# Sums over chunks in the FFN's down product, seeded in PSUM, in a two-layer diffusion backbone

## Chip, cores and metric

One Trainium2 chip, one core of it. The metric is device time in microseconds, the median of three runs; lower is better.

## What is computed

The input is a latent sequence of 512 tokens and a context of 256, both 1024 wide. Two layers run over them: an FFN half-step, a mixing of tokens (two kinds of attention and a Fourier mixing between an input and an output projection), and another FFN half-step. The same weights act on context and latent tokens; only the latent tokens are the output, so the last FFN leaves the context out. The FFN, to which the change belongs:

```python
def swiglu(h, w1, w2):
    gate, up = jnp.split(h @ w1, 2, axis=-1)
    return (jax.nn.silu(gate) * up) @ w2

def ffn_sublayer(h, m, sub, g_pre, g_post, w1, w2):
    shift, scale, gate = mods_of(m, sub)
    y = swiglu(modulate(rms_norm(h, g_pre[sub]), shift, scale), w1, w2)
    return h + MACARON_WEIGHT * gate * rms_norm(y, g_post[sub])
```

The inner width is 2816. `shift`, `scale` and `gate` come from a product of a conditioning vector with `w_mod` (1024 x 9216 in each layer).

## The kernel before

All matrix products run in three parts: both operands are split into a rounded high part and the rest, and high x high, high x rest and rest x high are added in PSUM (`mm`, L690 to L699). So each weight tile costs a copy on ScalarE (ACT; `wh`, L324) and a subtraction on VectorE (DVE; `wl`, L328) after its load.

The FFN takes its 22 pairs of 128 inner columns in seven chunks (`CHUNKS`: six of 3 pairs and one of 4). For each pair it computes gate and up. Two or three pairs of an FFN run plainly (`pair`); the others (`pair7`) form a two-by-two block product from seven products instead of eight, in three banks A, B and E. Between those products ACT copies a bank to SBUF (`copy`, L935) before the next product may go on in it, and DVE adds the pieces up (L941, L948, L968). After the pairs of a chunk and one more pair come the chunk's down products (`down`): for each tile of 128 tokens and each half of the output (12 tiles, or 8 without the context) 3 x 3 matmuls of 512 columns into one bank. Then `yacc` adds the bank to the tile y in SBUF: for the first chunk a copy on ACT (L1021), for the others an add on DVE (L1023). In the last chunk the tiles go on to the norm and the next stage (`chain`).

The modulation vectors are made beside all this: `mods` loads `w_mod` in 128 pieces (raw<-wmodT, L427) and multiplies them on DVE (L433), one or two products for each piece. When the eight pieces of a gate are done, `make_post` writes it as a row to DRAM (gsd<-gs, L533), element by element; from there it is read back as a broadcast. Loads of weights (raw<-w) and of w_mod (raw<-wmodT) and these rows are all issued by SyncE and share its DMA queue. The three `raw` buffers hold the loads until they are split or multiplied.

The order of all instructions is made ahead, when the kernel is built. `Sched` plays generators against a small model of the engines: an `op` occupies an engine for a given time, a `wait` waits for an event, an `acq` takes a slot of a counted resource (banks are `pb`, 8 of them; weight slots `w`), lower `prio` goes first where two could start together. `S.busy[engine]` is the time up to which an engine is occupied in that account. The order that it finds is what each engine's queue holds; on the chip an engine works it off in that order, and waits where something is not ready yet. A bank is a new tile of an eight-buffer pool each time (`bank`, L262).

Of the kernel before, what the change touches and what calls it, by code (L numbers as in the profile page):

```python
# [10 lines left out]
F32 = mybir.dt.float32  # L11
# [29 lines left out]
SCALE_ACT = 0.2  # L41
HALVES = ((1, 1),)
# [140 lines left out]
class Prog:  # L183
# [5 lines left out]
    def setup(self, es):  # L189
# [10 lines left out]
        self.pb = pool("pb", 8, space=PSUM)  # L200
# [3 lines left out]
        cp = self.cp  # L204

# [56 lines left out]
    def bank(self):  # L262
        p = self.pb.tile([128, 512], F32, name="b")
        return p
# [177 lines left out]
    def first_mods(self):  # L442
# [28 lines left out]
        def finish(j, ps):  # L471
            row = self.qp.tile([128, 512], F32, name="q")
            yield op("act", t_act(512), lambda: nc.scalar.activation(row[:4, :], ps[:4, :], AF.Copy))
            S.rel("pb")
# [11 lines left out]
            if j == 3:  # L486
                S.rel("pb")
# [77 lines left out]
    def chain(self, gi, src, post, pre, out=False):  # L565
# [86 lines left out]
        def split(j, bank):  # L652
# [10 lines left out]
            S.rel("pb")  # L663
# [48 lines left out]
    def ffn(self, l, f, streams, nxt):  # L712
# [19 lines left out]
        def evac(i, parts):  # L732
# [8 lines left out]
            def part(gate, up, banks, lo, n, ready, e):  # L741
# [4 lines left out]
                S.rel("pb", banks)  # L746
# [20 lines left out]
        def parts2(ps, ready):  # L767
            out = [(*ps["l"], 2, NC, NL, ready["l"], Event())]
            if has_c:
                out.append((*ps["c"], 1, 0, NC, ready["c"], Event()))  # L770
            return out
# [145 lines left out]
        def pair7(i):  # L917
# [6 lines left out]
            def out():  # L924
# [13 lines left out]
                def silu(h, src, p):  # L938
# [3 lines left out]
                    S.rel("pb")  # L942
# [3 lines left out]
                def store(h, up):  # L946
                    yield wait(gate[h])
                    yield op("dve", t_dve(N), lambda: nc.vector.tensor_tensor(ts[h], ts[h], up, ALU.mult))  # L948
                    S.rel("q" if h else "pb")
# [61 lines left out]

        ydone = {}

        def yacc(t, h, p, c, e, prio=None):
# [9 lines left out]
            S.rel("pb")  # L1024
            S.set(e)

        def down(c):
# [4 lines left out]
            def part(bank, t, h, ks, rel):  # L1032
                for k in ks:
                    w = yield wait(self.W["w2", l, f, c0 + (n * h + k) // 2][(n * h + k) % 2])
                    gt = [x[:, t * 128 : t * 128 + 128] for x in g[c0 + k]]
                    yield op("pe", 3 * t_mm(512), lambda: self.mm([bank], gt, [w], k == 0, k == n - 1))
                    if rel:
                        S.rel("w")

            for i in range(c0, min(c0 + n, NPAIR - 1)):  # L1040
                yield wait(gdone[i])
            if not last:
                for h in range(2):
                    for t in tiles:
                        yield acq("pb")
                        bank = self.bank()
                        yield from part(bank, t, h, range(n), t == tiles[-1])
                        S.spawn(yacc(t, h, bank, c, Event()), 2)
            else:
# [5 lines left out]
                first = [(t, h) for t in tiles[:2] for h in range(2)]  # L1055
                banks = {}
                for th in first:
                    yield acq("pb")
                    banks[th] = self.bank()
                    yield from part(banks[th], *th, range(n - 1), False)  # L1060
                for t in tiles:
                    yield wait(last_half[t % 2])
                    for h in range(2):
                        if (t, h) in banks:
                            yield from part(banks[t, h], t, h, [n - 1], False)
                        else:
                            yield acq("pb")
                            banks[t, h] = self.bank()
                            yield from part(banks[t, h], t, h, range(n), t == tiles[-1])
                        S.spawn(yacc(t, h, banks[t, h], c, evs[t, h]), 1 + 0.01 * t)  # L1070
# [3 lines left out]
        for c in range(len(CHUNKS)):  # L1074
            need = sum(CHUNKS[: c + 1])
            while made < min(need + 1, NPAIR):
                if made == NSTD[2 * l + f]:
# [3 lines left out]
            yield from down(c)  # L1081


    def mix(self, l, ctx_out, nxt):
# [27 lines left out]
        def evac(name, pl, pc, rels):  # L1112
# [10 lines left out]
            for r in rels:  # L1123
                S.rel(r)
            T[name] = t
            if n2 in ("av", "bv"):
                offs = [0, 128] + [NC + o for o in ((0, 128, 256, 384, 64, 192, 320) if n2 == "av" else (0, 128, 256, 384))]
                dst = self.va[:, :, int(name[2]) * 128 : int(name[2]) * 128 + 128] if n2 == "av" else self.vb
                for i in range(0, len(offs), 3):
# [7 lines left out]
                    S.rel("pb")  # L1137
# [21 lines left out]
        def u_split(c, outs):  # L1159

            for src, lo, hi in reversed(list(zip(outs, (NC, 0), (NT, NC)))):
# [4 lines left out]
                S.rel("pb")  # L1166
# [23 lines left out]
        def fnet():  # L1190
# [19 lines left out]
            def ab_split(tt, pb, e):  # L1210
# [3 lines left out]
                S.rel("pb")  # L1214
# [37 lines left out]
            S.rel("pb")  # L1252
            freed(0, 1)

            def unfold(s, c, h, a0, P, Q, banks):
# [7 lines left out]
                S.rel("pb", banks)  # L1263
                yield from out_split(s, 6 + c, f, ["q"])

            for s, i, h, tts, n in streams:
# [6 lines left out]
                for c in range(2):  # L1273
                    banks = 1 if s == "c" else 2
                    yield acq("pb", banks)
                    p = self.bank()
# [578 lines left out]
```

## Time and profile before

| | us |
|---|---|
| median of three runs | 2559.97 |
| lowest, highest | 2559.94, 2564.85 |
| the profiled execution | 2558.9 |
| its span (first to last instruction) | 2557.1 |

| engine | busy, us | share of the span |
|---|---|---|
| PE (TensorE, matmuls) | 2497.7 | 98% |
| DVE (VectorE) | 1956.6 | 77% |
| ACT (ScalarE) | 1265.7 | 49% |

Two matmuls overlap at their ends, so a busy PE is not a PE at its peak; what it lost shows as idle time, as a wait or as a lower granted clock. "b" is a bank, "g" the inner activations, "hh" and "hl" the two parts of the normed input, "x" tiles hold block sums. A line such as `ACT q L935 <- ...` names the engine, the tile that is written and the line of the kernel.

### The profile page before, as it was taken

Reading aid. Unit: us, or ns where it says so; the run is one execution under the profiler, and the core shown is the slowest. Engines: PE = TensorE matmul, PEld = TensorE weight load, DVE = VectorE, ACT = ScalarE, POOL = GpSimd, SP = SyncE. Lnnn points to the kernel's source line nnn. Section 1 sums busy time; section 2 is a strip of 40 time slices with the busy share of each in tenths; the row PEclk is TensorE's granted clock in tenths of the full one; section 3 lists DMA queues with packets and bytes.
Section 4 is the critical chain, followed back from the end, with each engine's and each line's share of the span. In section 5 each row is a group of like instructions: output and inputs, shape, how many; then the busy total and the mean of one; then the engine's idle time right before and its main releaser. Section 6 shows DMA issues by size and latency. Waiting matters only on the chain.

```text
span 2557.1 us, 40296 instructions
## 1 busy us (share of the span) xinstructions
PE 2497.7 (98%) x15304; PEld 2282.2 (89%) x15304; DVE 1956.6 (77%) x3906; ACT 1265.7 (49%) x2529; POOL 68.4 (3%) x136
## 2 busy tenths in 40 slices
PE   7999999999998999998999999999999999999998
PEld 5989998998887999998999999999999888899998
DVE  7878888876888397887887978666667686777887
ACT  8443333356657474333334643333347666654544
POOL 0000000010000000000000100000001000000000
PEclk9999999999999999999999999999999999999999
DMA  7344434353321334344447354222243222333333
GB/s 257 95 121 124 125 122 102 123 194 106 124 63 35 124 100 131 114 126 107 125 125 203 118 156 154 77 75 66 75 140 127 68 70 75 115 108 91 102 105 132
DMA packets 100931, 294.17 MB, mean 115 GB/s; under 512 B 20608, under 2 KB 27136, under 8 KB 100608
## 3 DMA queue, kind: packets, MB, share of 16 engines
q1 hardware_dynamic: 100736, 291.59, 37.1%
q8 instruction: 120, 1.97, 0.3%
q14 instruction: 75, 0.61, 0.1%
HBM read 274.73 MB, written 16.82 MB: 114 GB/s over the span
## 4 chain that ended last, share of the span: by engine, by line
PE 90%; DVE 4%; DMA 3%; ACT 2%; issue 1%; POOL 0%; SPq 0%; DVEq 0%; POOLq 0%; ACTq 0%
PE b L693 83%; PE b L1348 2%; PE b L1391 2%; PE b L1324 2%; DMA raw<-wmodT 1%; PE b L675 1%; DMA raw<-w 1%; DVE wl L328 1%; ACT wh L324 1%; DMA raw<-win 1%; DVE q L433 0%; DVE wl L460 0%; DVE g L1299 0%; ACT y L661 0%; PE b L499 0%
## 5 line engine op out<-in xcount | busy, mean ns | idle before, releaser
L693 PE MATMUL b<-hh,wh 128*128 128x256 f32 (+2 forms) x2184 | 702.6, 322 | 18.2 <-ACT q L935 12.6
L693 PE MATMUL b<-hl,wh 128*128 128x256 f32 (+2 forms) x2184 | 686.0, 317 | 1.9 <-DVE hl L668 1.6
L693 PE MATMUL b<-hh,wl 128*128 128x256 f32 (+2 forms) x2184 | 666.7, 318 | 0.0
L693 PE MATMUL b<-wh,g 128*128 128x512 f32 x1936 | 606.7, 390 | 0.0
L328 DVE TENSOR_TENSOR wl<-raw,wh 128x512 fp32r<-128x512 f32 x553 | 366.7, 688 | 128.8 <-ACT wh L324 126.5
L324 ACT ACTIVATE wh<-raw 128x512 fp32r<-128x512 f32 x553 | 336.3, 627 | 231.7 <-PE b L693 178.5
L693 PEld LDWEIGHTS b<-hh,wh 128*128 128x128 f32 x2184 | 413.8, 189 | 40.1 <-ACT q L935 13.5
L693 PEld LDWEIGHTS b<-wh,g 128*128 128x128 f32 x1936 | 363.5, 188 | 73.9
L693 PEld LDWEIGHTS b<-hl,wh 128*128 128x128 f32 x2184 | 413.7, 189 | 14.6 <-DVE hl L668 2.8
L693 PEld LDWEIGHTS b<-hh,wl 128*128 128x128 f32 x2184 | 401.6, 189 | 3.0
L324 ACT ACTIVATE wh<-q 128x512 fp32r<-128x512 f32 x308 | 190.6, 629 | 417.7 <-DVE y L1023 248.9
L693 PE MATMUL b<-wl,g 128*128 128x512 f32 x968 | 377.1, 390 | 0.0
L433 DVE CUSTOM_DVE_ANT_0 q<-raw,cb 128x1024 bf16<-128x1024 f32 x224 | 273.3, 1220 | 56.4 <-DMA raw<-wmodT 55.9
L693 PE MATMUL b<-x,wh 128*128 128x384 f32 (+1 forms) x1232 | 292.3, 323 | 0.0
L328 DVE TENSOR_TENSOR wl<-q,wh 128x512 fp32r<-128x512 f32 x308 | 206.2, 687 | 73.2 <-ACT wh L324 72.0
L1023 DVE TENSOR_TENSOR y<-y,b 128x512 f32<-128x512 f32 x264 | 179.4, 684 | 100.9 <-PE b L693 99.3
L693 PEld LDWEIGHTS b<-x,wh 128*128 128x128 f32 x1232 | 215.1, 189 | 0.0
L693 PEld LDWEIGHTS b<-wl,g 128*128 128x128 f32 x968 | 181.7, 188 | 36.0
L693 PE MATMUL b<-x,wl 128*128 128x384 f32 (+1 forms) x616 | 198.5, 322 | 0.0
L693 PE MATMUL b<-g,wh 128*128 128x384 f32 (+1 forms) x616 | 147.8, 325 | 3.5 <-ACT s L935 3.5
L961 ACT ACTIVATE g<-s 128x384 fp32r<-128x384 f32 (+1 forms) x154 | 75.5, 494 | 95.2 <-DVE s L948 94.0
L693 PEld LDWEIGHTS b<-x,wl 128*128 128x128 f32 x616 | 116.1, 189 | 0.0
(258 smaller groups left out, 3186.5 us busy)
## 6 DMA issues: line engine op xcount, KB each, us to landing
raw<-w SPq DMA_DIRECT2D x264, 512.0 KB, 3.7
raw<-wmodT SPq DMA_DIRECT2D x128, 512.0 KB, 3.6
raw<-win SPq DMA_DIRECT2D x32, 512.0 KB, 3.6
spill<-x SPq DMA_DIRECT2D x28, 512.0 KB, 2.9
x<-spill SPq DMA_DIRECT2D x26, 512.0 KB, 7.0
g<-wmod SPq DMA_DIRECT2D x32, 256.0 KB, 5.4
raw<-wout SPq DMA_DIRECT2D x16, 512.0 KB, 3.6
y<-bias SPq DMA_DIRECT2D x24, 256.0 KB, 3.2
```

The lines of the kernel that those rows point to most:

```text
L324: yield op("act", t_act(512), lambda: nc.scalar.activation(w[0], src, AF.Copy))
L328: yield op("dve", t_dve(512), lambda: nc.vector.tensor_tensor(w[1], src, w[0].bitcast(F32), ALU.subtract))
L433: yield op("dve", t_dve(1024, True), lambda: nc.vector.tensor_tensor_reduce(junk, raw, self.cb[:, i, :], 1.0, 0.0, ALU.mult, ALU.add, self ...
L675: r = nc.tensor.transpose(bank[:, c : c + 128], yb[:, t, 2 * j + i, :], self.ident)
L693: mm = lambda *a, **k: self.nc.tensor.matmul(*a, skip_group_check=onto, **k)
L961: yield op("act", t_act(N), lambda: nc.scalar.activation(gh, ts[h], AF.Copy))
L1023: yield op("dve", t_dve(512), lambda: nc.vector.tensor_tensor(dst, dst, p, ALU.add))
L1324: r = nc.tensor.transpose(pb[:, j * 128 : j * 128 + 128], P[:, b * 128 : b * 128 + 128], self.ident)
L1348: r = nc.tensor.matmul(ps[b][:, c : c + w], lhsT=q[x], rhs=k[x], start=first, stop=final, skip_group_check=True)
L1391: r = nc.tensor.matmul(po["t"][64 * h : 64 * h + 64, cols], lhsT=vs[h][j], rhs=Ps[h][:, j * 128 : j * 128 + 128], start=(j == 0), stop=(j ...
```

## The change

The sum over chunks goes through the bank. A generator `begin` runs ahead of the down products, at most two tiles (four in the last chunk): it takes a bank and, from the second chunk on, lets ACT copy y's part into it. The first matmul then adds to the bank's content, without its start flag. Afterwards the bank holds the sum and is copied to y, by ACT or by DVE. A tile is seeded only where ACT's account is at most 1.5 us (`ACT_MORE`) ahead of DVE's, and only in a bank that the down products have written in full before (`full`); otherwise the add on DVE stays. `plan` starts `begin` ahead of the last pair that precedes a chunk's down products.

The eight banks are made once and given out from a list of free ones: the down products prefer banks that are full, all others those that are not, in order of the time at which they came free. All places that gave back a count now give back the bank itself (`drop`); these lines are left out of the diff below.

```diff
+ACT_MORE = 1.5
-        self.pb = pool("pb", 8, space=PSUM)
+        self.pb = pool("pb", 1, space=PSUM)
...
+        self.banks = [self.pb.tile([128, 512], F32, name=f"b{i}") for i in range(8)]
+        self.bank_of = {b.tensor.name: i for i, b in enumerate(self.banks)}
+        self.free = [(0.0, i) for i in range(8)]
+        self.full = [False] * 8
...
-    def bank(self):
-        p = self.pb.tile([128, 512], F32, name="b")
-        return p
+    def bank(self, full=False):
+        self.free.sort(key=lambda e: (self.full[e[1]] != full, e))
+        i = self.free.pop(0)[1]
+        if not full:
+            self.full[i] = False
+        return self.banks[i]
+
+    def drop(self, *aps):
+        t = self.S.cur.t
+        for a in aps:
+            self.free.append((t, self.bank_of[a.tensor.name]))
+        self.S.rel("pb", len(aps))
...
+        def begin(c, order, look, evs):
+            for t, h in order:
+                yield acq(look)
+                yield acq("pb")
+                bank = self.bank(True)
+                i = self.bank_of[bank.tensor.name]
+                seeded = c > 0 and self.full[i] and S.busy["act"] <= S.busy["dve"] + ACT_MORE
+                if seeded:
+                    yield wait(ydone[t, h])
+                    yield op("act", t_act(512), lambda: nc.scalar.activation(bank, self.y[t][:, h * 512 : h * 512 + 512], AF.Copy))
+                self.full[i] = True
+                S.set(evs[t, h], (bank, seeded))
...
             if c == 0:
                 yield wait(y_free)
+            if c > 0 and not seeded:
+                yield op("dve", t_dve(512), lambda: nc.vector.tensor_tensor(dst, dst, p, ALU.add))
+            elif S.busy["act"] <= S.busy["dve"] + ACT_MORE:
                 yield op("act", t_act(512), lambda: nc.scalar.activation(dst, p, AF.Copy))
             else:
-                yield op("dve", t_dve(512), lambda: nc.vector.tensor_tensor(dst, dst, p, ALU.add))
-            S.rel("pb")
+                yield op("dve", t_dve(512), lambda: nc.vector.tensor_copy(dst, p))
+            self.drop(p)
...
+        def plan(c):
+            if c < len(CHUNKS) - 1:
+                order = [(t, h) for h in range(2) for t in tiles]
+            else:
+                order = [(t, h) for t in tiles for h in range(2)]
+            look = ("look", l, f, c)
+            S.res[look] = Res(2)
+            evs = {th: Event() for th in order}
+            S.spawn(begin(c, order, look, evs), 2)
+            return order, look, evs
...
-                    yield op("pe", 3 * t_mm(512), lambda: self.mm([bank], gt, [w], k == 0, k == n - 1))
+                    yield op("pe", 3 * t_mm(512), lambda: self.mm([bank], gt, [w], k == 0 and not seeded, k == n - 1, seeded))
                     if rel:
                         S.rel("w")
+                if ks[-1] == n - 1:
+                    S.rel(look)
...
+                S.rel(look, 2)
...
             while made < min(need + 1, NPAIR):
+                if made == min(need, NPAIR - 1):
+                    planned = plan(c)
```

## Rows read from the trace of the kernel before

**Rows 1.** The page: the span and the engines' busy time.

```profile
span 2557.1 us, 40296 instructions
...
PE 2497.7 (98%) x15304; PEld 2282.2 (89%) x15304; DVE 1956.6 (77%) x3906; ACT 1265.7 (49%) x2529; POOL 68.4 (3%) x136
```

**Rows 2.** Busy time by stretch: PE, PEld, DVE, ACT, POOL, then clock, DMA, GB/s.

```profile
250.40:318.80 68.40, 68.40 (x363) 64.14 (x362) 58.06 (x101) 25.57 (x48) 0.00 (x0) 1.00 0.41 123
250.40:276.80 26.40, 26.40 (x121) 22.22 (x120) 22.38 (x38) 5.02 (x9) 0.00 (x0) 1.00 0.32 100
276.80:318.80 42.00, 42.00 (x243) 41.92 (x242) 35.69 (x64) 20.56 (x40) 0.00 (x0) 1.00 0.47 138
...
2341.00:2387.30 46.30, 46.30 (x326) 43.43 (x325) 37.40 (x69) 22.90 (x48) 0.00 (x0) 1.00 0.34 102
```

**Rows 3.** The adds of L1023: ns min/median/max, first start; busy in one stretch.

```profile
L1023 DVE TENSOR_TENSOR y<-y,b x264: 677/684/690, 184.4 to 2549.8; 128x512 f32<-128x512 f32 x132
...
250.40:276.80 26.40, 7.53 (x11) 1.00 0.32 100
```

**Rows 4.** PE's waits, whole span: us in total, times, longest.

```profile
PE b L693 <- ACT q L935: 12.6, 3, 6.6
```

**Rows 5.** Busy time by stretch, as in rows 2, around three waits.

```profile
165.00:185.00 20.00, 15.62 (x77) 14.79 (x76) 11.21 (x21) 6.68 (x15) 0.00 (x0) 0.91 0.56 164
420.00:440.00 20.00, 16.48 (x86) 16.16 (x86) 17.26 (x30) 7.63 (x15) 0.00 (x0) 0.91 0.42 129
1200.00:1220.00 20.00, 13.38 (x68) 13.06 (x67) 16.64 (x28) 6.57 (x13) 0.00 (x0) 0.83 0.40 110
```

**Rows 6.** The chain of waits before each of the four: start, duration, what.

```profile
164.38 9.88 DMA raw<-w
...
409.68 12.38 DMA raw<-wmodT
...
1181.83 14.82 DMA raw<-wmodT
...
1206.96 0.60 DVE y L1023
...
1607.99 11.06 DMA raw<-w
```

**Rows 7.** The page: DMA issues, count, size, median us to landing.

```profile
raw<-w SPq DMA_DIRECT2D x264, 512.0 KB, 3.7
```

**Rows 8.** Stores of gate rows: issue ns min/median/max, start us.

```profile
L533 SPq DMA_DIRECT2D gsd<-gs00c x1: 391/391/391, 156.6 to 156.6; - x1
...
L533 SPq DMA_DIRECT2D gsd<-gs01c x1: 377/377/377, 400.7 to 400.7; - x1
...
L533 SPq DMA_DIRECT2D gsd<-gs02c x1: 377/377/377, 720.6 to 720.6; - x1
...
L533 SPq DMA_DIRECT2D gsd<-gs10c x1: 378/378/378, 1178.9 to 1178.9; - x1
...
L533 SPq DMA_DIRECT2D gsd<-gs11l x1: 413/413/413, 1388.7 to 1388.7; - x1
L533 SPq DMA_DIRECT2D gsd<-gs12l x1: 378/378/378, 1605.6 to 1605.6; - x1
```

**Rows 9.** ACT's copies of 512 columns: ns min/median/max.

```profile
L1021 ACT ACTIVATE y<-b x44: 578/598/601, 109.8 to 2266.9; 128x512 f32<-128x512 f32 x44
...
L324 ACT ACTIVATE wh<-raw x553: 612/632/642, 31.9 to 2530.0; 128x512 fp32r<-128x512 f32 x185
```

**Rows 10.** ACT's waits: in the stretch 250.4 to 276.8; in the whole span.

```profile
ACT wh L324 <- DVE y L1023: 9.5, 1, 9.5
...
ACT wh L324 <- DMA raw<-w: 37.5, 32, 8.7
```

**Rows 11.** Loads of w_mod from 250 to 319; their products on DVE (page).

```profile
L427 SPq DMA_DIRECT2D raw<-wmodT x7: 327/328/328, 255.1 to 312.3; - x7
...
L433 DVE CUSTOM_DVE_ANT_0 q<-raw,cb 128x1024 bf16<-128x1024 f32 x224 | 273.3, 1220 | 56.4 <-DMA raw<-wmodT 55.9
```

More of the change, by code (lines that the diff above doesn't have):

```diff
@@ L486, in finish @@
             if j == 3:
-                S.rel("pb")
+                self.drop(pt)
         S.spawn(loads(), 0)
@@ L662, in split @@
                         yb[:, :, k, :], src, AF.Identity, bias=sh[:, k : k + 1], scale=a[:, k : k + 1]))
-            S.rel("pb")
+            self.drop(bank)
             ks = slice(2 * j, 2 * j + 2)
@@ L1030, in down, with part @@
             last = c == len(CHUNKS) - 1
-            def part(bank, t, h, ks, rel):
+            def part(t, h, ks, rel):
+                bank, seeded = yield wait(banks[t, h])
                 for k in ks:
@@ L1042, in down @@
             if not last:
[L1043 to L1048, printed above, removed]
+                for t, h in order:
+                    bank, seeded = yield from part(t, h, range(n), t == tiles[-1])
+                    S.spawn(yacc(t, h, bank, c, seeded, Event()), 2)
             else:
@@ L1054, in down @@
                     S.spawn(self.chain(gi, evs, *nxt), self.prio[self.groups[gi]])
-                first = [(t, h) for t in tiles[:2] for h in range(2)]
-                banks = {}
+                first = order[:4]
+                S.rel(look, 2)
                 for th in first:
[L1058 to L1061, printed above, removed]
+                    yield from part(*th, range(n - 1), False)
+                for t, h in order:
                     yield wait(last_half[t % 2])
[L1063 to L1070, printed above, removed]
+                    if (t, h) in first:
+                        bank, seeded = yield from part(t, h, [n - 1], False)
+                    else:
+                        bank, seeded = yield from part(t, h, range(n), t == tiles[-1])
+                    S.spawn(yacc(t, h, bank, c, seeded, evs[t, h]), 1 + 0.01 * t)
             S.rel("g", 2 * n)
@@ L1080, in ffn @@
                 made += 1
-            yield from down(c)
+            yield from down(c, *planned)
     def mix(self, l, ctx_out, nxt):
@@ L1122, in evac @@
                 yield op("act", t_act(NC), lambda: nc.scalar.activation(t[:, :NC], pc, AF.Copy, scale=scale))
-            for r in rels:
-                S.rel(r)
+            self.drop(*rels)
             T[name] = t
@@ L1262, in unfold @@
                 yield op("dve", t_dve(h), lambda: nc.vector.tensor_tensor(f[:, 1:h], f[:, 1:h], Q[:, 1:h], ALU.subtract))
-                S.rel("pb", banks)
+                self.drop(*banks)
                 yield from out_split(s, 6 + c, f, ["q"])
@@ L1273, in fnet @@
                 for c in range(2):
-                    banks = 1 if s == "c" else 2
-                    yield acq("pb", banks)
-                    p = self.bank()
-                    P, Q = p[:, : h + 2], (p[:, 256 : 256 + h] if s == "c" else self.bank()[:, :h])
+                    yield acq("pb", 1 if s == "c" else 2)
+                    banks = [self.bank() for _ in range(1 if s == "c" else 2)]
+                    P, Q = banks[0][:, : h + 2], (banks[0][:, 256 : 256 + h] if s == "c" else banks[1][:, :h])
                     def positions(part, dst):
@@ L1665, in ycopy @@
             yield op("act", t_act(n), lambda: nc.scalar.activation(self.y[t][:, lo : lo + n], bank[:, :n], AF.Copy))
-            S.rel("pb")
+            self.drop(bank)
             if e is not None:
```

38 lines of the change are left out of this document (21 added, 17 removed).

## Prediction

> **What bounds the kernel now.** I read the page's busy shares first, then who TensorE (PE) waited for, then stretches of one chunk, and last the chain of work behind each wait.
>
> The busy shares [rows 1] make PE the bound: 2497.7 of 2557.1 us, with VectorE (DVE) at 77% and ScalarE (ACT) at 49%. So an edit that only moves work from DVE to ACT can give back PE's idle time, 59.4 us, and what PE's clock loses, and no more.
>
> The stretches of one chunk [rows 2] show how little of that lies in the FFNs. In the chunk from 250.4 to 318.8 us PE is busy for all 68.40 us at a granted clock of 1.00, although DVE is busy for 58.06 of them and ACT for 25.57. A chunk of the last FFN, at 2341.0, shows the same. In the stretch of the down products alone (250.4 to 276.8) DVE has 22.38 us of work, of which the adds that the change takes away are 7.53 [rows 3]; ACT has 5.02. PE never waits there. So DVE, the engine that the change relieves, is busy but not late.
>
> PE's waits [rows 4] name the exception, the longest in total: "ACT q L935", three times, 12.6 us. That is the copy of a product inside `pair7`, on which the next product of the same bank waits. Windows around three waits of this kind [rows 5] leave PE idle for 4.38 (165 to 185), 3.52 (420 to 440, there by the sister copy into s) and 6.62 us (1200 to 1220); the third copy to q is left with 12.6 - 4.38 - 6.62 = 1.6, at 1619. In all 16.1 us. The three windows also show a granted clock of 0.91, 0.91 and 0.83 over 20 us, so after the wait PE ran a while at 1.2 instead of 2.4 GHz. With that the dearest costs more than its wait: 68 matmuls in 20 us, where the pair stage of an undisturbed chunk does 243 in 42.0 [rows 2], or 116 in 20; 48 missing at 0.173 us (42.0 / 243) are 8.3 us. The one at 420 does 86: 30 x 0.173 = 5.2 us. The first costs 4.38 and 9% of 20 us, 6.2; the last 1.6. All four together are some 21 us, 0.8% of the time: that is the most that the FFN's engines hold back.
>
> Why they happen is in the chains behind them [rows 6]. Each leads through ACT or DVE to one late transfer: raw<-w 9.88 us, raw<-wmodT 12.38, raw<-wmodT 14.82, raw<-w 11.06. The median of such a load is 3.7 [rows 7]. Shortly before each stands the issue of a gate row, gsd<-gs [rows 8]: at 156.6, 400.7, 1178.9 (each a double row: one for the context, shown, and one for the latent tokens some 4 to 6 us later) and 1605.6 (single). I read from this that PE's FFN waits are made by weights and modulation loads standing behind gate-row stores in the DMA queue, with DVE or ACT held in order behind the late load. They are not made by too much DVE work.
>
> **The change part by part.** *PE.* No matmul more or less: the first of a seeded tile runs without its start flag, otherwise the same. 0 us.
>
> *DVE to ACT.* 264 adds of 684 ns [rows 3] fall away where a tile is seeded: up to 179.4 us of DVE. Each seeded tile costs ACT one copy into the bank. No row of before has ACT writing to a bank; the nearest are the copy of a bank to y (median 598 ns) and of an SBUF tile to wh (632) [rows 9]. I take 0.6; the bounds are 0.58 and 0.64 (the fastest of the one, the slowest of the other). The copy back is another 0.6 on ACT, or about 0.68 on DVE when ACT is ahead by 1.5 us in the planner's account. All on ACT: 264 x 1.2 = 317 us, ACT 1266 to 1583 us (62%), DVE 1957 to 1777. In the down stretch ACT goes from 5.02 to 5.0 + 12 x 1.2 = 19.4 of 26.4 us, DVE from 22.4 to 14.9. Both still fit. On PE's path: 0, while the seeds stay ahead.
>
> *The new wait.* PE's first matmul of a tile now waits for ACT, where before it waited for a free bank only. A tile takes nine matmuls; the down stretch does 121 in 26.40 us [rows 2], so nine in 1.96. Two tiles are in the look-ahead: a bank's copy back (0.6) and its next seed (0.6) have 2 x 1.96 = 3.9 us until PE comes to that tile, so the margin is 3.9 - 1.2 = 2.7 us; a weight copy of 0.63 between them leaves 2.1. In a steady chunk what ACT waits for in the down stage is PE itself: the 9.5 us put down to "DVE y" ended with PE's release of a w2 slot, since those adds came from PE too [rows 10]. Behind that wait the queue holds only work that is planned for later than the slot. Cost 0; from below no gain, from above what rival C tells.
>
> *Banks.* Eight named tiles with a list of free ones, in place of the pool's turn. No PE wait of rows 4 is for a bank, so nothing is to be won; a full bank is taken again after one copy instead of after seven others, which is the cover that the margin above counts. 0 us.
>
> *What a freed DVE starts.* Twelve adds at 0.60 us apiece (what one takes in the chains of rows 6) are 7.2 us a chunk. The modulation products (L433, 1220 ns, two to a load) fill what DVE has left: seven loads in that chunk [rows 11]. 7.2 us are room for three more (3 x 2 x 1.22 = 7.3), so the gate rows get ready earlier: not the first (it is issued at 156.6, before the first add at 184.4), but the second perhaps 60 us sooner, the third perhaps inside the first FFN instead of at 720, those of the second layer 50 to 100 us sooner. So the first wait stays as it is. The other three move to other places in the 68 us of a chunk, each as likely to hurt as before: two double rows cost 5.2 and 8.3 us, the single one 1.6, and the one from 720 may join them (+5) or be hidden. I keep their sum.
>
> What changes for sure is the backlog: of the chain before the wait at 1204 two adds of 0.60 us are part (one is shown) [rows 6]. Without them that wait is 1.2 us shorter; for the one at 420 the chain has no add. I take -2 us for all the moved waits together, between 0 and -4.
>
> *Ends of the FFNs and of the kernel.* The last tile's add (0.68) stands between PE and the end [rows 3]; it becomes a copy of 0.60 on ACT [rows 9]: -0.1 us. At the three other ends DVE and ACT are about even in load and a copy goes to the one less ahead: 0, between -1 and +2.
>
> Sum: 2558.9 (the profiled execution, span 2557.1 and 1.8 around it) - 2 - 0.1, or 2557. The median of the three runs is 2560.0 (2559.9 to 2564.9), so this is 0.1% below it.
>
> **A rule that speaks against it.** The rows first: with eight banks in turn the down stretches show clock 1.00 and no PE wait [rows 2]. The Trainium skill, TensorE: Matmul & The Clock Gate, section "A second HAM failure mode: psum-queue depth-cycling", tells of a kernel whose PE paused shortly between groups of matmuls while it cycled through PSUM banks, so that its clock went up and down. The trace of before agrees only in that a clock drop follows a PE pause, as at 1200; no run here shows it for short pauses. By that rule a rotation of three or four banks is the danger, and rival D is what it would do.
>
> **The rivals.** *A, forecast, 0.48:* as above, 2557, itself within 2550 to 2564.
>
> *B, the moved waits disappear, 0.20.* The gate rows land in stretches where PE needs no late load. For it: the single row at 1388.7, issued in a down stage, has no PE wait beside it in rows 4. Against it: the other stores inside FFNs all hurt, two of them issued in a down stage too. It gives 5.2 + 8.3 + 1.6 = 15 us: 2544.
>
> *C, slower: ACT is held in a down stage, 0.22.* A weight copy that stands before a seed in ACT's queue waits for a late load; before, PE had banks enough not to feel it. ACT's waits for raw<-w reach 8.7 us, 37.5 in total [rows 10]. It decides where ACT is held over 2.7 us while PE is in the down products. Price: 8.7 - 2.7 = 6.0 us and 1.8 of clock (the 0.91 over 20 us), 7.8 each; two hits among the four or five gate rows left make +16: 2575. Against it: in rows 2 and 10 no steady chunk has ACT held there by a load.
>
> *D, a short wait in every chunk, 0.05:* the 24 chunks with adds each lose 0.6 us, one copy, and 1.8 of clock: +58, 2617. It decides where a seed comes later than PE in the steady chunk. Against it: the 2.7 us margin.
>
> *E, few seeds, 0.05:* the planner finds ACT too far ahead and leaves the add on DVE in most tiles: 2559, no change.
>
> **How the numbers follow.** The range takes A whole, most of B and the nearer half of C: 2542 to 2575. A measurement can tell about 0.2% from no change, that is under 2554.9 or over 2565.1. Faster: nearly all of B, a quarter of A, 0.32. Slower: nearly all of C and D, 0.26. Within: 0.42.
>
> **What would show it.** Right: DVE near 1780 to 1850 us, ACT over 1450, PE's 15304 matmuls unchanged; no PE wait on the seed's line in a steady chunk; L935 still the main PE wait in the FFNs, each behind a gsd store, the first still near 172 and the others earlier than now. Wrong: a PE wait on the seed (C where few and long, D where many and short), all L935 waits gone (B), or over half of the adds still there (E). The forecast falls if the modulation loads do not get faster, since then the waits stay where they are and only the backlog counts.

## The result, and the profile after

| | before | after |
|---|---|---|
| median of the runs, us | 2561.21 (2559.94 to 2564.85, four runs) | 2582.23 (2577.2 to 2584.38, four runs) |
| ratio after / before | | 1.0077, 95% 1.0058 to 1.0096 |
| the profiled execution, its span, us | 2558.9, 2557.1 | 2583.3, 2581.5 |

The change makes the kernel 0.8% slower. The forecast was 2557.0 with a range up to 2575; the median lies 25 us above the one and 7 us above the other.

The page of the kernel after, span and busy time of each engine (to be laid beside [rows 1]):

```profile
span 2581.5 us, 40294 instructions
...
PE 2507.5 (97%) x15304; PEld 2289.9 (89%) x15304; DVE 1849.1 (72%) x3730; ACT 1479.5 (57%) x2926; POOL 59.5 (2%) x136
```

The work moved as planned: DVE has 107.5 us less, ACT 213.8 more, and PE runs the same 15304 matmuls. But PE is busy 9.8 us longer with them, and idle 14.6 us longer (74.0 instead of 59.4): together the 24.4 us of the span. The longer busy time goes with the clock: the stretches that the trace shows at half clock add up to 37.6 us before and 68.4 after. (24.4 us is the difference of the two profiled executions, which the following takes apart; the medians lie 21.0 us apart.)

The instructions that the change adds, and what is left of the old add (groups of the page and of DVE's lines: operation, shape, count, busy us, mean ns, idle time before them and its cause):

```profile
L1060 ACT ACTIVATE y<-b 128x512 f32<-128x512 f32 x221 | 130.9, 595 | 202.1 <-PE b L710 201.6
L1046 ACT ACTIVATE b<-y 128x512 f32<-128x512 f32 x221 | 128.4, 591 | 14.9 <-DVE y L1062 7.1
...
L1062 DVE COPY y<-b 128x512 f32<-128x512 f32 x44 | 30.3, 688 | 104.4 <-PE b L710 104.4
L1058 DVE TENSOR_TENSOR y<-y,b 128x512 f32<-128x512 f32 x43 | 29.1, 683 | 9.7 <-PE b L710 9.7
```

221 of 264 tiles are seeded (b<-y, L1046); 43 adds remain; 44 of the 265 copies back run on DVE. So rival E is out at once.

A steady chunk, and its down products alone (windows with the columns of [rows 2]; the chunk is the one that stood at 250.4 before):

```profile
253.30:321.70 68.40, 68.40 (x363) 64.14 (x362) 55.51 (x101) 37.58 (x69) 0.00 (x0) 1.00 0.40 123
253.30:279.70 26.40, 26.40 (x121) 22.20 (x120) 17.85 (x30) 14.77 (x26) 0.00 (x0) 1.00 0.32 100
```

It takes 68.40 us as in [rows 2], with PE busy throughout at a clock of 1.00. Seeding costs nothing here. So where do 24.4 us come from? The matmuls of the down products give marks at which the two traces can be compared: the first matmul of each chunk's down products, chunk 0 to 6 of the four FFNs, 0.0 to 3.6. The differences between two marks tell where a kernel lost or won. This table is worked out from the matmul starts in the traces (us, each kernel minus before; the kernels of the experiments are in it already, and "again" is the kernel before profiled a second time):

```
stretch                            after    e1    e2    e5    e6    e9  again
start to 0.0                        -0.6  -0.7  -0.9  +0.6  +0.4  -0.1  -0.8
0.0 to 0.1  (stores gs00c, gs00l)   +3.5  +0.1  +3.7  -6.0  -6.0  +2.7  -0.1
0.1 to 0.5  (stores gs01c, gs01l)   +2.0  +0.8  +0.6  -5.0  -5.1  +3.1  -0.3
end of 0.6 to 1.0, first mixing     +5.0  +4.9  +6.1  -1.2  +5.7  +4.0  -0.4
1.0 to 1.4  (stores gs10c, gs10l)   +2.7  +0.1  -1.1  -8.2  -8.3  +2.6  -0.1
1.4 to 1.6  (store gs11l)           +7.8  +0.0  -0.0  -0.0  +0.1  -0.0  +0.0
1.6 to 2.2  (store gs12l)           -1.4  +0.8  -0.6  -0.7  -1.3  -1.4  -0.5
end of 2.6 to 3.0, second mixing    +5.4  +1.7  +3.6  +0.5  +2.6  +2.8  +0.7
all other stretches                  0.0   0.0   0.0   0.0   0.0   0.0   0.0
whole span                         +24.4  +7.8 +11.4 -19.9 -11.8 +13.6  -1.5
```

In the first column two places stand out. Inside the FFNs 14.0 us, all of it in the few chunks beside a store of a gate row, none in the others. In the two mixing stages, where nothing is seeded, 10.4 us. Each column is one execution. "again" stays within 0.8 us of before, and e9, which leaves the three pairs of rows in the FFNs as the kernel after has them, repeats their pieces within 1.1 us.

TensorE's waits in the whole span of the kernel after (us in total, times, longest; the first belongs to the kernel's start):

```profile
PE b L516 <- ACT wh L476: 10.3, 1, 10.3
PE b L710 <- DVE q L988: 7.3, 1, 7.3
PE b L710 <- ACT q L952: 6.7, 1, 6.7
PE b L710 <- ACT b L1046: 5.7, 2, 5.1
PE b L710 <- ACT s L952: 5.4, 1, 5.4
```

The single wait with three hits of [rows 4] has become four different ones: two on the copies inside `pair7` (L952), one on DVE's addition of a bank to a block sum there (L988), and one on the seed itself (L1046: 5.1 us that end at 411.7, and 0.6 at 1200). The windows around them and the transfers at which the chains end:

```profile
165.00:185.00 20.00, 13.27 (x62) 12.95 (x61) 9.76 (x18) 6.16 (x12) 0.00 (x0) 0.74 0.77 158
390.00:424.00 34.00, 28.91 (x122) 23.77 (x121) 19.48 (x36) 14.93 (x27) 0.00 (x0) 0.90 0.54 90
1176.00:1220.00 44.00, 36.00 (x157) 30.50 (x156) 23.37 (x42) 19.96 (x36) 0.00 (x0) 0.88 0.45 99
1370.00:1390.00 20.00, 14.63 (x72) 14.31 (x71) 10.72 (x19) 7.56 (x15) 0.00 (x0) 0.83 0.53 87
```

```profile
165.05 11.34 DMA raw<-w
...
397.17 11.94 DMA raw<-wmodT
...
1176.88 18.68 DMA raw<-w
...
1369.17 13.02 DMA raw<-w
```

The third transfer belongs to the 0.6 us at 1200. The 7.3 us on L988, which ended at 1189.2, hang on another load, raw<-w issued at 1173.7, which took 12.9 us; ACT's weight copies waited for it and DVE's subtractions for them:

```profile
1186.68 1.15 ACT L341 ACTIVATE wh<-raw 128x512 fp32r<-128x512 f32 x2 [10.84 <-DMA raw<-w]
...
1187.34 1.29 DVE L345 TENSOR_TENSOR wl<-raw,wh 128x512 fp32r<-128x512 f32 x2 [9.40 <-ACT wh L341]
1188.55 0.55 DVE L988 TENSOR_TENSOR q<-q,b 128x384 f32<-128x384 f32 x1
```

Each wait hangs on one load that took 11 to 19 us, where the median is 3.7 as in [rows 7], and each stands right behind a store of a gate row (issues by SyncE; the first four are followed within 7 us by their latent row):

```profile
L550 SPq DMA_DIRECT2D gsd<-gs00c x1: 381/381/381, 156.6 to 156.6; - x1
...
L550 SPq DMA_DIRECT2D gsd<-gs01c x1: 377/377/377, 389.0 to 389.0; - x1
...
L550 SPq DMA_DIRECT2D gsd<-gs02c x1: 377/377/377, 682.3 to 682.3; - x1
...
L550 SPq DMA_DIRECT2D gsd<-gs10c x1: 377/377/377, 1173.3 to 1173.3; - x1
...
L550 SPq DMA_DIRECT2D gsd<-gs11l x1: 377/377/377, 1368.7 to 1368.7; - x1
L550 SPq DMA_DIRECT2D gsd<-gs12l x1: 377/377/377, 1592.2 to 1592.2; - x1
```

Against [rows 8] the rows are issued 0, 12, 38, 6, 20 and 13 us earlier by the clock of the trace. The work around them comes later in the kernel after, by 2.9 us at 0.4, 9.9 at 1.3, 12.6 at 1.5 and 20.9 at 2.1; against it the four in FFNs that moved come some 15, 15, 33 and 34 us earlier. In the profile this was enough to change what stands beside them: the single row gs11l, which cost nothing at 1388.7, at 1368.7 holds PE for the 5.4 us on L952; gs12l, with a wait at 1619 before, now has none.

### The profile page after: what moved, and what is told of

Same layout as the page of the kernel before. It is cut to its first block, busy times and chain, and to the rows that moved or that the text cites. A ratio compares the mean times of both kernels' runs of the same rounds, so it can differ in the third digit from the quotient of the medians.

```text
span 2581.5 us, 40294 instructions
## 1 busy us (share of the span) xinstructions
PE 2507.5 (97%) x15304; PEld 2289.9 (89%) x15304; DVE 1849.1 (72%) x3730; ACT 1479.5 (57%) x2926; POOL 59.5 (2%) x136
## 4 chain that ended last, share of the span: by engine, by line
PE 89%; DVE 4%; DMA 4%; ACT 3%; issue 1%; SPq 0%; POOL 0%; DVEq 0%; POOLq 0%; ACTq 0%
PE b L710 82%; PE b L1371 2%; DMA raw<-w 2%; PE b L1438 2%; PE b L1395 2%; PE b L692 1%; DMA g<-wmod 1%; DVE wl L345 1%; ACT wh L341 1%; DMA raw<-win 1%; DMA raw<-wmodT 0%; ACT y L678 0%; ACT hh L684 0%; DVE g L1346 0%; PE b L1182 0%
## 5 line engine op out<-in xcount | busy, mean ns | idle before, releaser
L341 ACT ACTIVATE wh<-raw 128x512 fp32r<-128x512 f32 x553 | 335.4, 627 | 233.3 <-PE b L710 156.7
L341 ACT ACTIVATE wh<-q 128x512 fp32r<-128x512 f32 x308 | 190.2, 629 | 152.4 <-DVE q L350 87.4
L1060 ACT ACTIVATE y<-b 128x512 f32<-128x512 f32 x221 | 130.9, 595 | 202.1 <-PE b L710 201.6
L1046 ACT ACTIVATE b<-y 128x512 f32<-128x512 f32 x221 | 128.4, 591 | 14.9 <-DVE y L1062 7.1
L350 DVE TENSOR_TENSOR q<-raw 128x512 f32<-128x512 f32 x154 | 105.5, 685 | 15.1 <-DMA raw<-w 15.1
```

What stands on the lines that cost most here:

```text
L341: yield op("act", t_act(512), lambda: nc.scalar.activation(w[0], src, AF.Copy))
L350: return op("dve", t_dve(512), lambda: nc.vector.tensor_tensor(o, a, b, f))
L1046: yield op("act", t_act(512), lambda: nc.scalar.activation(bank, self.y[t][:, h * 512 : h * 512 + 512], AF.Copy))
```

## The experiments

The theory at this point (T1): the FFN loses only by late loads behind gate-row stores; the new order of instructions moves the stores, and their sum is a matter of where each falls. The rivals: seeds come late (C), and the named banks cost by themselves, above all in the mixing stages (N).

**The banks alone, and everything but the seeds.** e1 is the kernel before with the eight named banks, their list and `drop`, and nothing else; the order of the instructions on every engine is that of before. e2 is the kernel after without seeds.

```diff
 e1 (before.py)
-        p = self.pb.tile([128, 512], F32, name="b")
-        return p
+        self.free.sort(key=lambda e: (self.full[e[1]] != full, e))
+        i = self.free.pop(0)[1]
...
 e2 (after.py)
-                seeded = c > 0 and self.full[i] and S.busy["act"] <= S.busy["dve"] + ACT_MORE
+                seeded = False
```

> The kernel before with the eight named banks and the list of free ones, first come first served, and nothing else of the change: no seeds, no look-ahead, the adds stay on DVE. Of the 24.4 us that the changed kernel's span is longer, 14 lie in the FFNs, each piece beside a gate-row store, and 10 in the two mixing stages, where nothing is seeded. Theory 1, the seeds cause the FFN part and the bank list causes the mixing part: about 2571, with both mixing stages 5 us longer. Theory 2, the mixing stages are longer only because all their work is planned at another time, and the bank list is free: 2561, within 3.

Measured: 2565.11 us against 2559.87, ratio 1.0017 (1.0007 to 1.0027). In the table the FFNs stay within about 1 us, which is what the second profile of the same kernel shows too, and the mixing stages lose 4.9 and 1.7 us, against -0.4 and +0.7 there. The window of the first mixing stage, first of e1, then of the kernel before in its second profile:

```profile
540.00:950.00 410.00, 397.70 (x2947) 352.63 (x2946) 310.29 (x819) 258.74 (x561) 28.45 (x62) 0.98 0.31 97
```

```profile
540.00:950.00 410.00, 400.01 (x2980) 354.73 (x2979) 314.34 (x828) 261.92 (x569) 28.40 (x62) 1.00 0.31 97
```

In the same 410 us e1 does 33 matmuls less: PE waits 2.3 us longer, and the clock is at 0.98 instead of 1.00. Two of the waits of e1 there that the kernel before does not have:

```profile
PE b L1411 <- DVE mx L1319: 2.1, 2, 1.4
...
PE b L1368 <- DVE s L1353: 1.0, 1, 1.0
```

So banks given out by name cost a little, although the work stands in the same order on each engine, and in these two profiles the cost lies in the mixing stages. N holds, for 5.2 us by the medians and 6.6 by the profiles. Neither forecast met the number: 2571 counted 5 us for each mixing stage, 2561 nothing.

> The changed kernel with no tile seeded: named banks, the preference for full banks and the early taking of two banks stay; the adds of the second to the last chunk stay on DVE, the first chunk's copy goes to the engine that is less ahead. Theory 1 (seeds make the FFN part): the FFN pieces at the second, the fourth and the fifth store fall away and 10 us of the mixing remain, about 2571. Rival (banks that are taken early and kept for the down products hold up the pairs): as slow as the changed kernel, 2580, with PE waits at the pairs.

Measured: 2568.27, ratio 1.0030 (1.0017 to 1.0043). Without a single seed the stretch of the first store still costs 3.7 us more than before. The down products of 1.3 take 33.4 us instead of 26.8, with a wait of 4.5 us on DVE's add (L1058), and the pairs behind them win that back. The mixing stages cost 6.1 and 3.6. So part of the loss in the FFNs comes with the order that the look-ahead makes, not with seeds. The pieces at the second, the fourth and the fifth store did fall away, as theory 1 had it; whether the seeds had made them or the moved rows, e2 can't tell. That is left to e6 and e9.

**The stores, made harmless.** If the stores of the gate rows are the cause, another form of the same store must take the waits away. PE transposes the row in a bank, 128 x 8 to 8 x 128, and the row goes out as eight runs of 512 bytes instead of 1024 single elements. e3 is the kernel before with it, e4 the kernel after.

```diff
-            yield op("sp", 0.4, lambda: nc.sync.dma_start(out=row.rearrange("o (k p) -> p (o k)", p=128), in_=g), 2.0)
+            yield acq("pb")
+            bank = self.bank()
+            yield op("pe", 0.1, lambda: nc.tensor.transpose(bank[:KT, :128], g, self.ident))
+            yield acq("q")
+            gt = self.qp.tile([128, 512], F32, name="q")[:KT, :128]
+            yield op("act", 0.2, lambda: nc.scalar.activation(gt, bank[:KT, :128], AF.Copy))
...
+            yield op("sp", 0.4, lambda: nc.sync.dma_start(out=row.rearrange("o (k p) -> (o k) p", p=128), in_=gt), 2.0)
```

> The kernel before, with a gate row turned by PE into 8 partitions of 128 values and stored as 8 runs of 512 bytes, not as 1024 elements of 4 bytes. If the late loads behind PE's FFN waits are made by the element-wise stores, the four waits go with what the clock loses: 2561 - 21 = 2540, and the loads beside the rows land in about 4 us. Rival (the loads are late for another reason, such as two reads at once): 2561, waits as before.

Measured: 2568.72, ratio 1.0033 (1.0020 to 1.0046): slower, not faster. The FFN's waits behind stores did go: -6.2, -5.3, -8.5 and -1.8 us at the four places. But the rows went too: e3 issues its ten from 552.7 on, none of them in the chunks that lost time before. So e3 shows that the waits hang on the stores, and not yet that their form matters. `make_post` runs at the planner's priority 8 and now needs a bank, which it was not given until 553 us, the end of the first FFN; and that end waits for the row:

```profile
PE b L683 <- DVE y L643: 17.6, 4, 16.4
...
545.00:600.00 55.00, 33.42 (x213) 29.95 (x212) 35.19 (x65) 28.71 (x61) 6.17 (x8) 0.75 0.36 125
```

The first line is PE's wait in 530 to 620, the second the window of that end. PE waits 16.4 us in one go and has a clock of 0.75; in all 31.1 us are lost before the next FFN.

> The changed kernel with the same 512-byte gate rows. Theory (a seed costs only where a late load holds ACT or DVE): the FFN part of the difference vanishes, so this is 2540 + 0 to 10 of the mixing stages, 2540 to 2550, and no PE wait for a seed is left. Rival (seeds on ACT cost PE by themselves): the FFNs stay 14 us longer than in the kernel before with the same rows, 2554 or more.

Measured: 2569.54, ratio 1.0036 (1.0024 to 1.0049), with the same two sides: -6.2, -5.3, -8.5, -1.8 in the FFNs, +26.6 at the end of the first. Both forecasts, 2540 and 2540 to 2550, fail on that end; for the seeds e4 says as little as e3 for the form, as its rows too are issued outside those chunks.

**The same with a priority that finds a bank.** e5 is e3, e6 is e4 with

```diff
-            S.spawn(self.make_post(*k), 8)
+            S.spawn(self.make_post(*k), -1)
```

> The kernel before with 512-byte gate rows again, now with make_post ahead of all others in the planner. In e3 the four FFN waits were gone (the down products came 21.8 us sooner in all), but at priority 8 the turning of the first rows got no bank until 553 us, and the end of the first FFN waited 31 us for them. Without that delay: 2560 - 22 = 2538, down stages earlier by 6.2, 5.3, 8.5 and 1.8 us at the four places, mixing stages as before within 2. If the waits of e3 were only pushed to other places, it stays over 2555.

Measured: 2540.39 us against 2560.18, ratio 0.9921 (0.9901 to 0.9942): the fastest kernel of this study. The stretches behind its double rows, which e5 issues at 155.8, 396.8 and 1164.9 us (windows as in [rows 5]):

```profile
165.00:185.00 20.00, 20.00 (x108) 18.90 (x107) 16.63 (x29) 9.14 (x18) 0.00 (x0) 1.00 0.50 158
385.00:415.00 30.00, 30.00 (x146) 25.96 (x145) 26.40 (x48) 6.80 (x13) 0.00 (x0) 1.00 0.32 94
1165.00:1195.00 30.00, 30.00 (x149) 26.50 (x148) 24.99 (x45) 8.67 (x16) 0.00 (x0) 1.00 0.30 90
```

PE is busy for all of the 80 us, at full clock. The first double row stands where it stood, within a microsecond, so it is not its place that changed; and e6 (below), whose rows stand in the FFNs at other times again (157.6, 164.2, 380.6 and on), loses nothing behind them either. What changed is the packets. The DMA view of 150 to 190 us, first the kernel before, then e5 (the last column is the median time to landing):

```profile
DMA packets 3407, 4.84 MB, mean 121 GB/s; under 512 B 2234, under 2 KB 2234, under 8 KB 3404
...
gsd<-gs00c SPq DMA_DIRECT2D x1, 4.0 KB, 8.7
gsd<-gs00l SPq DMA_DIRECT2D x1, 4.0 KB, 10.7
```

```profile
DMA packets 1527, 5.48 MB, mean 137 GB/s; under 512 B 182, under 2 KB 198, under 8 KB 1524
```

And the landing times of the loads into `raw` in the same stretch, before and e5 (as far as the traces have them: all eight before, four of ten in e5):

```profile
DMA to landing us min/median/max: 3.5/4.5/11.5
```

```profile
DMA to landing us min/median/max: 3.5/4.0/4.1
```

The two rows of 4 KB were some 2050 packets of under 512 bytes (2234 - 182) and took 8.7 and 10.7 us to land; without these packets no load whose landing the trace has takes longer than 4.1 us there (nor than 6.0 anywhere in the span, by 150 of 392 loads), where the longest of before takes 11.5. That the others were not late either shows only in PE, which never waits. With e5 as the measure, the stores cost the kernel before 6.0 + 5.0 + 8.2 us (the table) and 1.7 for the single row gs12l (the stretch from 2.1 to 2.2 alone), 20.9 in all. The prediction read 6.2, 5.2, 8.3 and 1.6 out of waits and clock.

> The changed kernel with the same rows at the same priority. Theory (seeds cost only beside a late load; the bank list costs some 6 us in the mixing stages, as e1 showed): e5 + 5 to 10, 2543 to 2548, all of the difference in the mixing stages, all down stages of the FFNs without a PE wait. Rival (a seed costs something in each chunk): e5 + 14 or more, the difference grows inside the FFNs.

Measured: 2546.89, ratio 0.9947 (0.9932 to 0.9962). With harmless stores the change's FFNs run like those of e5, within 0.5 us in every chunk of all four. So seeds, look-ahead and copies on ACT cost nothing in the FFNs; what e6 loses against e5 are 6.9 and 2.0 us in the mixing stages (6.5 us by the medians, with four runs each that do not overlap). That is near what the banks cost alone in e1; how much of it the order adds is not separated. From the table, after minus e6, the stores cost the kernel after 9.5 + 7.1 + 11.0 + 7.7 = 35.3 us, 14.4 more than before.

**Is it late seeds?** e7 is the kernel after with twice the look-ahead, so that a seed has four tiles' time.

```diff
-            S.res[look] = Res(2)
+            S.res[look] = Res(4)
```

> The changed kernel with four tiles of look-ahead instead of two. If PE waits for a seed because ACT is held longer than two tiles last (2 x 2.04 us), four tiles (8.2 us) hide the wait of 5.3 us in the down products at 406 and most of what is lost at 1181 to 1200: some 5 to 10 us less than the changed kernel, 2572 to 2577. If the look-ahead is not what limits (ACT waits behind the late load already when the first two seeds are due, or the pairs miss the banks), it stays at 2580 or goes over.

Measured: 2584.09, ratio 1.0093 (1.0078 to 1.0108): no gain. The seed's wait is gone, but in the stretch from 385 to 420 the kernel after (first line) and e7 (second) show:

```profile
PE b L710 <- ACT b L1046: 5.1, 1, 5.1
```

```profile
PE b L710 <- ACT q L952: 5.5, 1, 5.5
```

The down products get 7.4 us shorter, and the pair before them 7.6 us longer; at the store of the second layer it is 5.7 and 6.1. The late load holds whichever step comes first. C's wait exists and is not what the time is lost to.

**Is it where the store falls?** e8 is the kernel before with each store planned 20 us later. The account's engine for that is shared, so a latent row behind its context row comes some 40 us later. In the trace the rows in the FFNs come 15 to 51 us later, and the two rows of a pair stand 30 to 34 us apart instead of 3 to 6. e9 is the kernel after with only gs11l planned 40 us later, which puts it into the last chunk's down products.

```diff
 e8 (before.py), ahead of the store
+            yield op("later", 20.0, lambda: None)
...
 e9 (after.py), ahead of the store
+            if (l, sub) == (1, 1):
+                yield op("later", 40.0, lambda: None)
```

> The kernel before with each gate-row store planned 20 us after its row is made, element by element as before; nothing else is changed by hand. Theory (where a store falls in a chunk decides what it costs, whatever the FFN's sums do): the four FFN waits of 4.4, 3.5, 6.6 and 1.6 us change by several us each, in both directions, and the total by up to 10: 2550 to 2570. Rival (a store costs the same wherever it falls): 2560 within 2.

Measured: 2564.51, ratio 1.0016 (1.0006 to 1.0027). Its profiled execution is the longest of the ten, so I use only the chunks beside stores. Against before they change by -4.5, +4.6, +7.0 and -1.8 us: with e5 as the measure, the first two rows cost 1.5 us instead of 6.0, the second two 9.6 instead of 5.0, the third two 15.2 instead of 8.2 and the single rows nothing. The forecast's rival, 2560, is out by the medians too. But place and distance of a pair's rows moved together, and the profiled execution took 7.0 us more than the median of the ten, which may sit in these very chunks; the sizes are those of one execution.

> The changed kernel with one store, the single row gs11l, planned 40 us later. In the changed kernel it is issued at 1368.7, beside pairs, and 7.8 us are lost there; in the kernel before it is issued at 1388.7, in the last chunk's down products, and nothing is lost. Theory (where a store falls decides): it falls near 1409 in the last down products, the 7.8 us come back, 2574; all else as in the changed kernel within 2. Rival (with seeds a store in the down products costs as much, since ACT holds the seeds up): 2582, with a PE wait for a seed near 1410.

Measured: 2573.50, ratio 1.0044 (1.0033 to 1.0055). The row is issued at 1403.1 instead of 1368.7, and the stretch 1.4 to 1.6 goes from +7.8 to 0.0. In the window where the kernel after has 14.63 us of PE at a clock of 0.83, e9 has:

```profile
1370.00:1390.00 20.00, 20.00 (x117) 20.00 (x116) 16.56 (x30) 10.92 (x22) 0.00 (x0) 1.00 0.54 165
```

So one row's place alone is worth 7.8 us (8.7 by the medians). What a place means can be read from SyncE's issues, first in the kernel after, then in e9:

```profile
1368.70 0.38 SPq L550 DMA_DIRECT2D gsd<-gs11l  x1
1369.17 0.53 SPq L332 DMA_DIRECT2D raw<-w  x1
1369.85 15.29 SPq L444 DMA_DIRECT2D raw<-wmodT  x2
```

```profile
1403.07 0.37 SPq L552 DMA_DIRECT2D gsd<-gs11l  x1
...
1425.94 8.90 SPq L332 DMA_DIRECT2D raw<-w  x4
```

In the kernel after two loads into `raw` follow the row within 1.2 us, and they take 13.0 and 13.6 us. In e9 the next one comes 22.9 us behind the row, in the kernel before 27.4 us; by then the row has landed (after 13.2 and 12.3 us), and nothing is lost. The other rows fit: of all loads into `raw` that are issued in the 5 us behind a row, the kernel before has 8, which take 9.9 to 14.8 us, and the kernel after 13, which take 9.4 to 18.7. Their number alone does not give the price: e8 has only 4 and loses 26.3 us. Nor does each such load cost: behind gs12l in the kernel after one takes 9.4 us, and PE does not wait.

The second mixing stage of e9 is 2.6 us shorter too, which no theory here had.

**Is it the choice of bank?** The list gives out the bank that came free first; the pool gave the banks in turn. e10 is e1, e11 is e6, with the bank that was given out longest ago.

```diff
-        self.free.sort(key=lambda e: (self.full[e[1]] != full, e))
+        self.free.sort(key=lambda e: (self.full[e[1]] != full, self.given[e[1]], e[1]))
         i = self.free.pop(0)[1]
+        self.gave += 1
+        self.given[i] = self.gave
```

> As e1 (named banks, no seeds), but a free bank is chosen by the longest time since it was last given out, not since it came free: the pool's turn. The order of all instructions stays that of the kernel before. Theory (the mixing stages lose some 6 us because a bank that came free first in the plan is often one whose reader is late on the chip, and a turn leaves it more time): 2560 within 2, mixing stages as before. Rival (named tiles bind reads and writes of one bank more tightly, whatever the choice): 2565, as e1.

> The changed kernel with 512-byte gate rows ahead of others (e6) and the choice of e10, full banks still first for the down products. If both costs of the change are those found (stores, and the choice of banks in the mixing stages), it equals e5: 2540 within 3. If the choice is not what the mixing stages lose, it stays at e6: 2547.

Measured: e10 2564.73, ratio 1.0012 (1.0003 to 1.0022); e11 2546.49, ratio 0.9939 (0.9922 to 0.9956). Neither is told apart from e1 and e6. The mixing stages lose 2.4 and 4.2 us in e10's profile, so neither of the two choices is what makes the cost. It moves between the two stages, and in the two profiles the sum stays at 6.6 us.

**The kernel before once more**, as a control for the small differences.

> The kernel before once more, unchanged, to see what the pieces differ by from one execution to the next. If the named banks cost the mixing stages by themselves, these differ here by under 1 us, and the +2 to +7 us of e1, e5 to e6 and e10 mean something; if they differ by 3 us or more here, these are the scatter of the mixing stages. The FFN pieces beside the stores should repeat within 1 us.

Measured: 2557.44 us in one run, the last column of the table: every stretch within 0.8 us of the first profile. That alone does not make differences of 2 to 7 us in a mixing stage more than scatter: another execution of the same kernel, on the same chip beside this one and without a trace, took 2572.04 us, and the 17 runs beside e10 go from 2556.4 to 2568.2. The two profiles of before are both in the lower half. What is clear of scatter are the medians: 1.0017 for e1 and 1.0012 for e10, both intervals above 1, and e5 against e6. That this cost lies in the mixing stages rests on the table, where the FFNs of e1 leave little room for it: their pieces add up to +1.8 us.

## Why the prediction was wrong, point by point

*What bounds the kernel*: right. Waits in the FFNs hang on late loads behind gate-row stores, not on DVE's load; e5 shows it, and its 20.9 us stand beside the 21 that were read from windows and clock.

*PE, the move to ACT, the new wait*: right, all 0. The copy into the bank takes 591 ns (0.6 taken), ACT comes to 1479.5 us and DVE to 1849.1, inside what was to be seen, and no steady chunk has a wait on the seed.

*Where the stalls go, "I keep their sum"*: this step failed, and it is the larger part of the miss. The text gave each moved store an equal chance to hurt as before and kept about 21 us; the stores of the kernel after cost 35.3 by the same measure (e6), 14 us more. e9 shows that a single row costs 0 or 7.8 us with its place, and in e8's one profile a pair costs between 1.5 and 15.2. A sum of four or five such draws was no quantity to keep; by these figures a range of some 20 us to the upper side is an estimate of what it needed. What the prediction did not ask is which loads are issued while a row is landing.

*"The first wait stays as it is"*: wrong too. Its row is issued at 156.6 in both kernels, but the latent row behind it 2.4 us later (162.7), and they cost 9.5 us instead of 6.0. e2 shows the same without seeds, so it is the new order around it.

*"Three more loads a chunk", rows 50 to 100 us sooner*: wrong. DVE has 55.51 us in the chunk instead of 58.06. With the two products of one more load (2 x 1.22) taken off that is 5.0 us less, not 7.2, and there are eight loads of w_mod instead of seven [rows 11], not ten:

```profile
L444 SPq DMA_DIRECT2D raw<-wmodT x8: 328/328/328, 257.3 to 320.1; - x8
```

The later rows moved by 6 to 38 us, or by 15 to 34 against the work around those in FFNs, not by 50 to 100. It was enough to change their places all the same. By the text's own sign (modulation loads no faster, so waits where they are) the waits should have stayed; they did not.

*"Banks. 0 us"*: wrong. The argument was that no wait of before was for a bank, so nothing could be won; it gave no price to a loss. e1 measures one: 0.17% (0.07 to 0.27), in its profile 6.6 us of mixing stages and little in the FFNs. Of the 10.4 us that the kernel after loses there, these are the greater part, if one execution may be set against another. The rest goes with the moved order (e2 has 9.7 without seeds; e9, with one row moved, has 2.6 less in the second), by a mechanism that stays open.

*Rival C* names a wait that came, but not its price, and for the longer of its two hits not its cause. The chain behind the seed's wait at 411:

```profile
397.17 11.94 DMA raw<-wmodT
...
409.14 0.04 DVE q L450
...
410.37 0.61 DVE y L1062
...
411.01 0.61 ACT b L1046
```

Here it is not ACT behind a weight copy, but DVE behind a modulation product: a copy back to y (L1062) that the planner had put on DVE stood in the queue behind it, and the seed waited for that copy. C's own cause, a weight copy on ACT that waits for a late load (wh, L341), stands in the chain behind the hit at 1200, which is 0.6 us. e7 then shows that the price is the late load's, not the seed's.

*Rival D*: out. The down products of every steady chunk run at clock 1.00 without a wait. The Trainium skill's rule that was weighed there (TensorE: Matmul & The Clock Gate, "A second HAM failure mode: psum-queue depth-cycling") does not show in them; how many banks in rotation it would take, "three or four", is the prediction's own reading, the page gives no number. In the mixing stages, where named banks cost time, e1's trace has 46 us at half clock in the whole span instead of 37.6, but whether pauses for banks start it, no run here separates.

*Rival B*, all stalls gone, is reached by e5 in another way: 2540.39, near its 2544. The row that spoke for B, gs11l at 1388.7, was harmless because no load into `raw` followed it for 27.4 us, which held for none of the rows that the change moved in the FFNs.

## What to carry to other kernels

A stall whose cause is a transfer belongs to the transfer, not to the engine that waits for it: relieving the engine leaves the stall, and in this kernel each change to the order of instructions drew its place and size anew. What it cost hung on the loads that were issued while it was under way. So price it at a range, or better remove its cause first; here some ten lines that store a row in runs of 512 bytes gave 0.8%, about as much as the change lost. And that nobody waits for a resource now says only that nothing can be won there; what holding it more tightly costs has to be bounded separately.

## What the runs showed of the hardware

- A store of 4 KB in single elements of 4 bytes took 8.7 to 19.5 us to land (before, after). The 21 loads of 512 KB that were issued within 5 us behind such a store took 9.4 to 18.7 us, where the median of raw<-w is 3.7. Behind the same 4 KB in runs of 512 bytes, the loads whose landing the traces of e5, e6 and e11 have took 3.4 to 4.8 us.
- Copying 512 columns from SBUF into a bank took ACT 591 ns on average, copying back 595. The Trainium skill (ScalarE: Activation LUTs, "Step-by-step: what each stage is for") has ACT faster into PSUM than into SBUF; here the difference is 4 ns, between copies whose sources differ too.
- The same instructions in the same order on each engine ran 0.17% slower with eight banks given out by name than with a pool in turn, and giving out the free bank that had rested longest did not undo it (e1; e10, 0.12%). Why is open.
